# A decoder step on one core: block sums on VectorE instead of GpSimd, squared relu on ScalarE, down products added into the residual rows as they come

## The chip, the core and the metric

The kernel runs on one core of one Trainium2 chip. The core has a matrix engine (TensorE, PE in the profile), VectorE (DVE), ScalarE (ACT) and GpSimd (POOL), each of which takes its own instructions in order; SyncE (SP) issues most transfers between the DRAM and the on-chip memory, in order as well. Matmuls write to PSUM, from which VectorE and ScalarE read. The metric is the device time of one execution in microseconds, the median over runs. Lower is better.

## The reference

One inference step of a decoder layer in fp32, for 1024 prompt tokens and 8 x 8 sample tokens, 1088 tokens in all. The part that matters here is the end of the layer and the output of the updated key and value buffers:

```python
h = x + jnp.einsum('btd,de->bte', mixed, w_o)                       # 1024 -> 1024
z = jnp.einsum('btd,df->btf', rms_norm(h, ln2), w_up)               # 1024 -> 4096
return h + jnp.einsum('btf,fd->btd', jnp.square(jax.nn.relu(z)), w_down)   # 4096 -> 1024
# and, for each of three head groups, the window of keys and values moved on by 8 rows:
kv_s[g].append(jnp.stack([k_full[:, T:], v_full[:, T:]], axis=2))
```

## The kernel before

The products are made of fp32 values split into a high and a low part (`split` and `put`: ScalarE copies the high part, VectorE subtracts it from the value to get the low part), and each product is three matmul passes: high by high, high by low, low by high. Before a matmul can use an operand, both instructions have to have run on it.

The kernel is one long program: input projection, attention and pooling up to about 420 us, gates and the two branch projections to about 660, then the three parts that the change touches.

*w_o.* Two halves of the tokens (`j` = 0, 1; 544 tokens each), each with four weight panels and eight output tiles `y[j][kk]`. Behind each tile its square is added into `sqa[j]`. The first half's norm is woven into the second half's products: the list `todo` has one entry taken behind every half of an output tile, and holds `norm_sums(0)` (matmuls `rth` with ones, then a power on GpSimd), `norm_spread(0)` (matmuls `bc`), the eight `normed` and the eight splits and stores to `u_d`.

*Up.* `w_up` is multiplied block-wise: rows and columns are cut in two, and 7 products of sums and differences of blocks take the place of 8 (the Strassen-Winograd form). `make_versions` makes the sums of activation blocks T1 to T4 from the normalised rows; the weight sums of each of the 16 groups `f` are made in `summed`. A group has 7 steps of 24 matmuls: p1 and p2 need only plain blocks, p5, p6, p7 and p4 need T1, T2, T3 and T4, p3 a plain block. The results of a group are combined, squared (`relu_squared`) and combined again into the seven operands that down wants, and stored to `z_d`. The first `FIRST` groups have their p1 and p2 ahead of everything else, since these need the first half's rows alone; the second half's norm (`norm_sums(1)`, `norm_spread(1)`, `make_versions`) hangs behind the first two of those steps.

*Down.* Seven stages, in the order 2, 4, 1, 5, 6, 7, 3, named after the product they make; each has 16 steps of 24 matmuls into four PSUM tiles (`pd`), which the next stage's first step needs again. A step takes a weight block `w` and a `z` tile. The stages 4 and 1 put their weights into `kept`, and the stages 5, 6, 7 and 3 make sums of blocks on GpSimd (`prep`). `post_down` takes the results out of PSUM behind a stage's last step: into `acs` and `vws` in the stages 2, 4, 1 and 5; behind 6 everything is combined and added to the residual rows `hs`, most of it on GpSimd; behind 7 and 3 the last product is added while the row is written in token order (`finish_row`), and the row is stored.

`run` writes up's and down's steps out: loads are issued 9 steps ahead, `prep` (sums and splits) 3 steps ahead of the matmuls, `post` behind them. PE keeps this order; for the other engines and the transfer queue a scheduler decides how the instructions are interleaved when the program is built. `raw_tile` has two buffers, and in down each holds two steps; five places in turn (`put_up`, `put_down`) hold the split operands, so a split can run as soon as the matmuls of five steps before are done. All loads and stores of these parts go through SP's one queue.

*Copies.* The move of the key and value buffers is 44 copies DRAM to DRAM, issued on GpSimd's queue. Each is made to wait for a mark: the split of a weight panel (`throttle`, one per panel; the last eight are the `w_o` panels) or of an up or down operand (`marks_f`, one per up step, two per down step). The marks are taken at equal distances in one list.

The lines of the profile to know: L1381 and L1382 are the high and low part in `put`, L114 and L115 those in `split`, L1450 the up matmuls, L1722 the down matmuls, L1502 the squared relu, L1540 the weight sums, L1636 the last addition into a row, L1742 the copies; on SP, L1686 loads `hs`, L1691 and L1693 `kept`, L1695 and L1696 `w` and `z`.

Of the kernel before, what the change touches and what calls it, by code (L numbers as in the profile page):

```python
# [32 lines left out]
FIRST = 3  # L33
# [3 lines left out]
def decoder_step(ctx, tc, i, o):  # L37
# [162 lines left out]
    z_d = dp.tile([NG, P, 7, H], F32, name="z_d")  # L200
    new_d = dp.tile([NT, NB, 768], F32, name="new_d")
# [1096 lines left out]
    y = [[pool_.tile([P, H], F32, name=f"y{j}_{k}") for k in range(KD)] for j, pool_ in enumerate((y0p, y1p))]  # L1298
# [34 lines left out]
    for j in range(2):  # L1333
# [32 lines left out]
    up2s = up2 = op = None  # L1366
# [37 lines left out]
    def make_versions():  # L1404

        nonlocal up2s, up2
        nps.close()
        fours = ups.enter_context(tc.tile_pool(name="t4", bufs=1, reuse_waits="tile"))
        sums_at[4] = tuple(fours.tile([P, 4, H], F32R, name=f"t4_{s}") for s in range(2))
        res, rep = right("again")  # L1410
        u12, u22 = y[1][:4], y[1][4:]

        def again(k):
            t = rr(rep, [P, H], F32, name=f"re{k}", tag="re", bufs=4)
            dma(t, u_d[k])
            return t

        def parts(n, k, f):
            hi, lo = (t[:, k, :] for t in sums_at[n])
            split(hi, lo, f)  # L1420

        u11 = [again(k) for k in range(4)]
        for k in range(4):
            normed(k, 1)
            v_.tensor_tensor(u11[k], u12[k], u11[k], op=ALU.subtract)
            parts(1, k, u11[k])
        for k in range(4):
            normed(4 + k, 1)
            split(act[0][4 + k][:, half(1)], act[1][4 + k][:, half(1)], u22[k])
            g_.tensor_tensor(u12[k], u22[k], u12[k], op=ALU.subtract)  # L1430
            v_.tensor_tensor(u22[k], u22[k], u11[k], op=ALU.subtract)
            parts(2, k, u22[k])
        u21 = [again(4 + k) for k in range(4)]
        for k in range(4):
            parts(3, k, u12[k])
        for k in range(4):
            g_.tensor_tensor(u21[k], u21[k], u22[k], op=ALU.subtract)
            parts(4, k, u21[k])
# [15 lines left out]
    queue = []  # L1454
# [8 lines left out]
    def run(ahead=3, load_ahead=9):  # L1463
        n_load = n_prep = 0
        got = {}
        for n in range(len(queue)):
            while n_load < min(len(queue), n + load_ahead):
                if queue[n_load][0]:
                    queue[n_load][0]()
                n_load += 1  # L1470
            while n_prep < min(len(queue), n + ahead):
                got[n_prep] = queue[n_prep][1]()
                n_prep += 1
            queue[n][2](got.pop(n))
            queue[n][3]()

# [30 lines left out]
    def group(f, early):  # L1507
# [11 lines left out]
        def first_post():  # L1519
            t = temp(1, f)  # L1520
            firsts[f] = [t, None, q["x"]]
            s_.copy(two(t), xs_of(q["x"]))  # L1522

        def second_post():
            t = temp(2, f)
# [11 lines left out]

        def summed(n, a, b, op):
            sums[n] = sum_tile(f"{n}_{f}")
            g_.tensor_tensor(by_tile(sums[n]), a, b, op=op)  # L1540
            return put_up(sums[n])

        def p5():
            def post():
# [4 lines left out]
                 lambda A: products(xt(), A, B["T1"], True), post, (lambda: load_panel(f)) if early else None)  # L1549
# [9 lines left out]
        def p7():  # L1559
            def post():  # L1560
# [3 lines left out]
                g_.tensor_tensor(q["s5"], u3, q["s5"], op=ALU.add)  # L1564
# [5 lines left out]
        def p3():  # L1570
            def post():
# [5 lines left out]
                g_.tensor_tensor(t1, z12, z11, op=ALU.subtract)  # L1577
# [3 lines left out]
                g_.tensor_tensor(z12, z22, z12, op=ALU.subtract)  # L1581
# [5 lines left out]
        def p4():  # L1587
            def post():
# [5 lines left out]
                g_.tensor_tensor(t4, z21, q["t2"], op=ALU.subtract)  # L1594
# [19 lines left out]
    kept, acs, vws, hs, rows = {}, {}, {}, {}, {}  # L1614

    def turn_over():
        nonlocal op
# [3 lines left out]
        op = ctx.enter_context(tc.tile_pool(name="down", bufs=1, side="right", reuse_waits="tile"))  # L1621
        for n in (1, 2):
# [5 lines left out]
    def out_row(t, kt, tag):  # L1628
        rows[kt] = op.tile([P, TOK], F32, name=f"row{kt}", tag=f"{tag}.{t}")

    def finish_row(kt, x, js):
        for j in js:
            if x is None:
                s_.copy(by_token(rows[kt], j), two(hs[kt][:, half(j)]))
            else:
                v_.tensor_tensor(by_token(rows[kt], j), two(hs[kt][:, half(j)]), xs_of(x), op=ALU.add)  # L1636

    def post_down(p, xs):
        for t in range(4):
            x = xs_of(xs[t])  # L1640
            if p == 2:
                acs[t] = op.tile([P, 2, H], F32, name=f"ac{t}", tag=f"ac.{t}")
                vws[t] = op.tile([P, 2, H], F32, name=f"vw{t}", tag=f"vw.{t}")
                s_.copy(two(acs[t][:, 0]), x)
            if p == 4:
                s_.copy(two(acs[t][:, 1]), x)
            if p == 1:
                s_.copy(two(vws[t][:, 1]), x)
                v_.tensor_tensor(two(acs[t][:, 0]), two(acs[t][:, 0]), x, op=ALU.add)
            if p == 5:  # L1650
                s_.copy(two(vws[t][:, 0]), x)
            if p == 6:
                a, c, v, w = acs[t][:, 0], acs[t][:, 1], vws[t][:, 0], vws[t][:, 1]
                v_.tensor_tensor(two(w), two(w), x, op=ALU.add)
                g_.tensor_tensor(v, v, w, op=ALU.add)
                g_.tensor_tensor(c, c, w, op=ALU.add)
                for kt, j, s in ((t, 0, a), (t, 1, v), (4 + t, 0, c), (4 + t, 1, v)):
                    (g_ if j else v_).tensor_tensor(hs[kt][:, half(j)], hs[kt][:, half(j)], s, op=ALU.add)  # L1658
                out_row(t, 4 + t, "ac")
                out_row(t, t, "vw")  # L1660
                finish_row(t, None, (0,))
            if p == 7:
                finish_row(4 + t, xs[t], (0, 1))
                dma_st(o["yT"][(4 + t) * P:(5 + t) * P], rows[4 + t])
            if p == 3:
                finish_row(t, xs[t], (1,))
                dma_st(o["yT"][t * P:(t + 1) * P], rows[t])
# [3 lines left out]
    def down_stage(p):  # L1671
# [10 lines left out]
        def load(f):  # L1682
            if f == 0 and p == 5:
                for kt in range(KD):
                    hs[kt] = op.tile([P, TOK], F32, name=f"hs{kt}")
                    dma(hs[kt], h_d[kt])  # L1686
# [11 lines left out]
        def prep(f):  # L1698
# [3 lines left out]
            elif p in (5, 6):  # L1702
                k1 = kept[1, f]
                if p == 5:
                    g_.tensor_tensor(k1, w, k1, op=ALU.add)
                else:
                    g_.tensor_tensor(k1, k1, kept[2, f], op=ALU.subtract)
                w = k1
            elif p == 7:
                g_.tensor_tensor(w, kept[2, f], w, op=ALU.subtract)  # L1710
            elif p == 3:
                g_.tensor_tensor(w, w, kept[1, f], op=ALU.subtract)
# [27 lines left out]
    late = throttle[13:] + marks_f[:-20]  # L1740
# [103 lines left out]
```

## Time and profile before

| | us |
|---|---|
| median of 3 runs (lowest, highest) | 1533.63 (1532.34, 1535.55) |
| the profiled execution, its own time | 1534.52 |
| its span | 1532.7 |
| PE busy in the span | 1459.3 |
| VectorE, ScalarE, GpSimd busy | 937.0, 647.1, 548.4 |
| first up matmul, first and last down matmul | 771.8, 1136.7, 1525.9 |
| mean clock granted to PE | 0.974 of full |

All times within the profile are microseconds from the start of the span, but for means of one instruction, which are in nanoseconds. A group line names line, engine, operation, output and inputs, shape and count, then busy time and mean, then the engine's idle time just before and who ended it. A wait line reads: who waited, for whom, total, times, longest. In a timeline line stand start, duration, the instruction merged with its like, and in brackets the idle time before the first; SPq is SP's queue, on which a transfer's duration is that of its issue and not of the move. A few per cent of the matmul records can be missing.

### The profile page before, as it was taken

Reading aid. Unit: us, or ns where it says so; the run is one execution under the profiler, and the core shown is the slowest. Engines: PE = TensorE matmul, PEld = TensorE weight load, DVE = VectorE, ACT = ScalarE, POOL = GpSimd, SP = SyncE. Lnnn points to the kernel's source line nnn. Section 1 sums busy time; section 2 is a strip of 40 time slices with the busy share of each in tenths; the row PEclk is TensorE's granted clock in tenths of the full one; section 3 lists DMA queues with packets and bytes.
Section 4 is the critical chain, followed back from the end, with each engine's and each line's share of the span. In section 5 each row is a group of like instructions: output and inputs, shape, how many; then the busy total and the mean of one; then the engine's idle time right before and its main releaser. Section 6 shows DMA issues by size and latency. Waiting matters only on the chain. (4 is left out here: it accounts for less than half of the span.)

```text
span 1532.7 us, 28345 instructions
## 1 busy us (share of the span) xinstructions
PE 1459.3 (95%) x10765; PEld 1399.9 (91%) x10765; DVE 937.0 (61%) x1550; ACT 647.1 (42%) x1802; POOL 548.4 (36%) x461
## 2 busy tenths in 40 slices
PE   9999999999999999998988999999999699999788
PEld 8988878888899999998977999999999699999788
DVE  7655575767746424255678766666663346967774
ACT  8567656787433222123342233233333244343331
POOL 1711355455100000000066766665630003825641
PEclk9999999999999999999988999999999799999889
DMA  5312787554354222397534655555579856665483
GB/s 198 107 45 92 215 222 197 146 134 112 112 161 148 81 100 97 100 299 256 207 121 143 213 193 172 192 188 177 196 249 382 309 170 204 221 211 191 163 271 120
DMA packets 160005, 272.69 MB, mean 178 GB/s; under 512 B 32311, under 2 KB 83837, under 8 KB 158142
## 3 DMA queue, kind: packets, MB, share of 16 engines
q1 hardware_dynamic: 153758, 220.56, 45.5%
q0 software_dynamic: 6112, 50.33, 9.9%
q8 instruction: 84, 1.38, 0.4%
q14 instruction: 51, 0.42, 0.1%
HBM read 211.90 MB, written 102.59 MB: 205 GB/s over the span
## 5 line engine op out<-in xcount | busy, mean ns | idle before, releaser
L1722 PE MATMUL pd<-places 128*128 128x272 f32 x2688 | 352.6, 294 | 36.6 <-ACT places L1381 19.9
L1722 PEld LDWEIGHTS pd<-places 128*128 128x128 f32 x2688 | 348.2, 195 | 40.9 <-ACT places L1381 21.7
L1382 DVE TENSOR_TENSOR places<-raw_d,places 128x544 fp32r<-128x544 f32 (+1 forms) x160 | 159.3, 1021 | 61.9 <-ACT places L1381 61.2
L1742 POOL DMA_DIRECT2D out_kv_sample_dram<-in_cache_kv_dram x44 | 22.8, 519 | 419.9 <-ACT places L114 193.5
L1381 ACT ACTIVATE places<-raw_d 128x544 fp32r<-128x544 f32 (+1 forms) x160 | 98.9, 642 | 118.1 <-DMA raw_d<-z_d 53.1
L1450 PE MATMUL pz<-act,places 128*128 128x272 f32 x984 | 133.8, 295 | 8.4 <-DVE act L115 4.3
L1450 PEld LDWEIGHTS pz<-act,places 128*128 128x128 f32 x984 | 130.2, 194 | 9.1 <-DVE act L115 4.7
L1382 DVE TENSOR_TENSOR places<-kept,places 128x512 fp32r<-128x512 f32 x64 | 55.6, 869 | 82.4 <-ACT places L1381 82.3
L184 PE MATMUL pga<-act,places 128*128 128x384 f32 (+1 forms) x576 | 100.2, 333 | 0.0
L184 PE MATMUL ph<-act,places 128*128 128x272 f32 x768 | 99.3, 292 | 0.6 <-ACT places L114 0.6
L184 PEld LDWEIGHTS ph<-act,places 128*128 128x128 f32 x768 | 98.6, 192 | 0.9 <-ACT places L114 0.8
L184 PE MATMUL pgb<-act,places 128*128 128x384 f32 (+1 forms) x576 | 97.9, 327 | 0.0
L184 PEld LDWEIGHTS pga<-act,places 128*128 128x128 f32 x576 | 96.2, 190 | 0.8 <-issue 0.3
L184 PEld LDWEIGHTS pgb<-act,places 128*128 128x128 f32 x576 | 95.4, 188 | 0.0
L599 POOL TENSOR_TENSOR mr<-ms,mhalf 128x4 f32<-128x4 f32 (+2 forms) x39 | 52.3, 1343 | 108.1 <-DVE ms L598 107.9
L1381 ACT ACTIVATE places<-kept 128x512 fp32r<-128x512 f32 x64 | 40.4, 632 | 114.3 <-PE pd L1722 73.4
L1450 PE MATMUL pz<-act,apart 128*128 128x272 f32 x552 | 74.2, 293 | 2.5 <-ACT t L1522 2.5
L1450 PEld LDWEIGHTS pz<-act,apart 128*128 128x128 f32 x552 | 72.2, 192 | 2.8 <-ACT t L1522 2.7
L1502 DVE SCALAR_TENSOR_TENSOR t<-t 128x544 f32<-128x544 f32 x48 | 55.2, 1150 | 18.8 <-POOL t L1564 18.8
L804 POOL TENSOR_TENSOR pck<-pck,qs 128x256 f32<-128x256 f32 x64 | 48.1, 783 | 43.0 <-DMA pck<-in_cache_kv_dram 17.5
L1540 POOL TENSOR_TENSOR sm<-raw_u 128x512 f32<-128x512 f32 x32 | 52.4, 1637 | 29.3 <-DVE places L1382 15.3
L184 PE MATMUL pqk<-places,act 128*128 128x512 f32 x240 | 61.0, 403 | 1.0 <-ACT qk L604 1.0
(371 smaller groups left out, 2922.5 us busy)
## 6 DMA issues: line engine op xcount, KB each, us to landing
out_kv_sample_dram<-in_cache_kv_dram POOLq DMA_DIRECT2D x36, 960.0 KB, 6.3
raw_d<-z_d SPq DMA_DIRECT2D x112, 272.0 KB
z_d<-t SPq DMA_DIRECT2D x96, 272.0 KB
raw_u<-in_w_up_dram SPq DMA_DIRECT2D x64, 256.0 KB
raw_d<-in_w_down_dram SPq DMA_DIRECT2D x64, 256.0 KB
raw_qkv<-in_w_in_dram SPq DMA_DIRECT2D x36, 256.0 KB
xr<-in_xT_dram SPq DMA_DIRECT2D x8, 1088.0 KB
pck<-in_cache_kv_dram SPq DMA_DIRECT2D x32, 256.0 KB
```

Of the source, the lines that this page charges most:

```text
L184: last_mm[0] = t_.matmul(out, lhs(a, k), rhs(b, k), start=(j == 0), stop=(j == len(terms) - 1))
L599: g_.tensor_tensor(r[:n, :H], ms[:n, :H], mhalf[:n, :H], op=ALU.pow)
L804: behind_pe(g_.tensor_tensor(t[:, n], t[:, n], qs[:, :256], op=ALU.mult))
L1381: ins = s_.activation(view(t[:, 0]), src, AF.Copy)
L1382: v_.tensor_tensor(view(t[:, 1]), src, view(t[:, 0]).bitcast(F32), op=ALU.subtract)
L1450: t_.matmul(x[:, c, :Q], A[:, a, k * P:(k + 1) * P], Bv(b, k, c), start=(first and n == 0), stop=(n == len(terms) - 1), skip_group_check=n ...
L1502: v_.scalar_tensor_tensor(t, t, 0.0, t, op0=ALU.max, op1=ALU.mult)
L1540: g_.tensor_tensor(by_tile(sums[n]), a, b, op=op)
L1722: t_.matmul(q["x"][t][:, c, :Q], A[:, a, t * P:(t + 1) * P], Z[:, b, c * Q:(c + 1) * Q], start=(f == 0 and n == 0), stop=(f == NG - 1 and ...
L1742: ins = g_.dma_start(d, a)
```

## The change

All sums of weight blocks and of results move from GpSimd to VectorE; the squared relu becomes two ScalarE passes. `FIRST` goes from 3 to 5; the early groups' two results are parked in `e` tiles, written out to `p_d` and `z_d` and read back when the group goes on. `make_versions` works on two blocks (1088 columns) at a time. The first half's norm is taken two half-tiles later, and its spread three. In down, `hs` is loaded beside the last eight steps of stage 2 instead of ahead of stage 5; the results are added to `hs` as they come, one addition behind a step (`later`), and `acs` and `vws` are replaced by `parked` and `running`. The marks of the copies count the panels several times, and down's marks singly and without the first 24.

```diff
-FIRST = 3
+FIRST = 5
...
+    p_d = dp.tile([FIRST, P, H], F32, name="p_d")
...
-            todo += [lambda: norm_sums(0), lambda: norm_spread(0)]
+            wait = lambda: None
+            todo += [wait, wait, lambda: norm_sums(0), wait, lambda: norm_spread(0)]
...
+        u12, u22 = fours[1]
+        u11 = rep.tile([P, 4, H], F32, name="u11")
+        pairs = (slice(0, 2), slice(2, 4))
+        def minus(out, a, b):
+            for k in pairs:
+                v_.tensor_tensor(out[:, k], a[:, k], b[:, k], op=ALU.subtract)
+        def parts(hi, lo, f):
+            for k in pairs:
+                split(hi[:, k], lo[:, k], f[:, k])
+        for k in range(4):
+            dma(u11[:, k], u_d[k])
         for k in range(4):
             normed(k, 1)
+        minus(u11, u12, u11)
+        parts(*sums_at[1], u11)
+        for k in range(4, 8):
+            normed(k, 1)
+        minus(u11, u22, u11)
+        parts(*sums_at[2], u11)
+        minus(u12, u22, u12)
+        parts(*sums_at[3], u12)
+        parts(plane(0, 1, 1), plane(1, 1, 1), u22)
         for k in range(4):
+            dma(u12[:, k], u_d[4 + k])
+        minus(u12, u12, u11)
+        parts(*sums_at[4], u12)
...
             queue[n][3]()
+            if later:
+                later.pop(0)()
...
-        return rr(up if n < 3 else up2, [P, H], F32, name=f"t{n}_{name}", tag=f"t{n}", bufs=FIRST if n < 3 else 1)
+        return rr(up if n < 3 else up2, [P, H], F32, name=f"t{n}_{name}", tag=f"t{n}", bufs=2 if n < 3 else 1)
+    def park(n, name):
+        return rr(up, [P, H], F32, name=f"e{n}_{name}", tag=f"e{n}", bufs=1)
     def relu_squared(t):
-        v_.scalar_tensor_tensor(t, t, 0.0, t, op0=ALU.max, op1=ALU.mult)
+        s_.activation(t, t, AF.Relu)
+        s_.activation(t, t, AF.Square)
...
+            if early:
+                dma_st(p_d[f], t)
...
+        def back():
+            load_panel(f)
+            for n, src in ((1, p_d[f]), (2, z_d[f, :, 0, :])):
+                firsts[f][n - 1] = temp(n, f"again{f}")
+                dma(firsts[f][n - 1], src)
         def summed(n, a, b, op):
             sums[n] = sum_tile(f"{n}_{f}")
-            g_.tensor_tensor(by_tile(sums[n]), a, b, op=op)
+            v_.tensor_tensor(by_tile(sums[n]), a, b, op=op)
...
-                g_.tensor_tensor(q["s5"], u3, q["s5"], op=ALU.add)
+                v_.tensor_tensor(q["s5"], u3, q["s5"], op=ALU.add)
...
+    def adds(kt, j, src):
+        return lambda: v_.tensor_tensor(hs[kt][:, half(j)], hs[kt][:, half(j)], src, op=ALU.add)
+    def row_half(kt, j, src):
+        v_.tensor_tensor(by_token(rows[kt], j), two(hs[kt][:, half(j)]), src, op=ALU.add)
...
+            v, w = parked[:, t], running[:, t]
+            if p in (2, 4):
+                kt = t if p == 2 else 4 + t
+                v_.tensor_tensor(two(hs[kt][:, half(0)]), two(hs[kt][:, half(0)]), x, op=ALU.add)
             if p == 1:
+                s_.copy(two(w), x)
+                later.append(adds(t, 0, w))
             if p == 5:
+                s_.copy(two(v), x)
+                later.extend((adds(t, 1, v), adds(4 + t, 1, v)))
             if p == 6:
                 v_.tensor_tensor(two(w), two(w), x, op=ALU.add)
+                later.extend((adds(4 + t, 0, w), adds(t, 1, w), adds(4 + t, 1, w)))
             if p == 7:
+                s_.copy(two(v), x)
+                new_row(4 + t)
+                later.append(lambda t=t, v=v: row_half(4 + t, 0, two(v)))
+                later.append(lambda t=t, v=v: (row_half(4 + t, 1, two(v)), row_done(4 + t)))
             if p == 3:
+                row_half(t, 1, x)
+                row_done(t)
+        if p == 7:
+            for t in range(4):
+                later.append(lambda t=t: (new_row(t), s_.copy(by_token(rows[t], 0), two(hs[t][:, half(0)]))))
...
-            if f == 0 and p == 5:
-                for kt in range(KD):
-                    hs[kt] = op.tile([P, TOK], F32, name=f"hs{kt}")
-                    dma(hs[kt], h_d[kt])
+            if p == 2 and f >= KD:
+                kt = f - KD
+                hs[kt] = op.tile([P, TOK], F32, name=f"hs{kt}")
+                dma(hs[kt], h_d[kt])
...
-                    g_.tensor_tensor(k1, w, k1, op=ALU.add)
+                    v_.tensor_tensor(k1, w, k1, op=ALU.add)
...
-    late = throttle[13:] + marks_f[:-20]
+    n_up = 7 * NG
+    late = [t for t in throttle[13:-8] for _ in range(4)] + [t for t in throttle[-8:] for _ in range(2)]
+    late += marks_f[:n_up] + marks_f[n_up + 24:-20:2]
```

The three other sums in `prep` (`kept[1]` less `kept[2]`, `kept[2]` less `w`, `w` less `kept[1]`) and the four other sums of results in up change their engine in the same way. `new_row` gives the rows `4 + t` and `t` the same buffer, so row `t` waits for the store of row `4 + t`.

More of the change, by code (lines that the diff above doesn't have):

```diff
@@ L1611, in decoder_step @@
                 p()
-    kept, acs, vws, hs, rows = {}, {}, {}, {}, {}
+    kept, hs, rows = {}, {}, {}
     def turn_over():
-        nonlocal op
+        nonlocal op, parked, running
         ups.close()
@@ L1621, in turn_over @@
         op = ctx.enter_context(tc.tile_pool(name="down", bufs=1, side="right", reuse_waits="tile"))
+        parked, running = (op.tile([P, 4, H], F32, name=n) for n in ("parked", "running"))
         for n in (1, 2):
@@ L1638, in post_down, with new_row, row_done @@
+    def row_half(kt, j, src):
+        v_.tensor_tensor(by_token(rows[kt], j), two(hs[kt][:, half(j)]), src, op=ALU.add)
+    def new_row(kt):
+        rows[kt] = op.tile([P, TOK], F32, name=f"row{kt}", tag=f"row.{kt % 4}")
+    def row_done(kt):
+        dma_st(o["yT"][kt * P:(kt + 1) * P], rows[kt])
     def post_down(p, xs):
+        assert not later
         for t in range(4):
             x = xs_of(xs[t])
[L1641 to L1644, printed above, removed]
```

76 lines of the change are left out of this document (15 added, 61 removed).

## The prediction

> **What bounds the kernel now.** I read the page's first part, then TensorE (PE) stage by stage, then what PE waited for.
>
> ```profile
> span 1532.7 us, 28345 instructions
> PE 1459.3 (95%) x10765; PEld 1399.9 (91%) x10765; DVE 937.0 (61%) x1550; ACT 647.1 (42%) x1802; POOL 548.4 (36%) x461
> ...
> 860.00:1100.00 240.00, 240.00 (x1913) 240.00 (x1913) 164.02 (x173) 74.81 (x124) 151.84 (x103) 1.00 0.54 183
> 1222.00:1292.00 70.00, 70.00 (x564) 70.00 (x564) 32.85 (x47) 29.55 (x51) 6.20 (x8) 1.00 0.57 188
> ...
> 771.80:826.30 54.50, 39.96 (x232) 37.95 (x231) 45.48 (x52) 24.13 (x42) 35.41 (x20) 0.78 0.42 138
> 1136.60:1185.30 48.70, 48.24 (x386) 47.85 (x384) 24.55 (x33) 17.74 (x30) 6.31 (x6) 1.00 0.98 355
> 1185.30:1256.00 70.70, 55.13 (x411) 54.31 (x411) 25.65 (x38) 25.76 (x44) 2.43 (x5) 0.88 0.71 251
> 1300.00:1353.00 53.00, 48.56 (x374) 47.94 (x373) 49.09 (x41) 19.59 (x34) 41.60 (x30) 0.97 0.65 217
> 1403.00:1466.00 63.00, 52.58 (x378) 51.30 (x378) 51.99 (x38) 21.32 (x32) 47.30 (x34) 0.92 0.54 180
> 1466.00:1525.90 59.90, 54.18 (x393) 52.88 (x392) 33.90 (x39) 16.64 (x28) 18.91 (x15) 0.89 0.52 171
> ...
> PE pd L1722 <- ACT places L1381: 19.9, 3, 11.5
> PE pz L1450 <- ACT t L1522: 6.5, 2, 4.1
> PE pd L1722 <- DVE row L1636: 5.7, 4, 2.8
> PE pd L1722 <- DVE places L1382: 4.5, 5, 2.5
> PE pd L1722 <- DVE ac L1649: 4.3, 2, 2.5
> PE pz L1450 <- DVE act L115: 4.3, 2, 3.7
> ...
> 721.85 2.03 PE L1309 MATMUL rth<-ones,sqa 128*128 128x1 f32 x10 [4.56 <-DVE sqa L1353]
> 723.81 5.31 PE L184 MATMUL ph<-act,places 128*128 128x272 f32 x24
> ...
> 774.81 1.14 PE L1309 MATMUL rth<-ones,sqa 128*128 128x1 f32 x10
> 779.24 1.16 PE L1322 MATMUL bc<-dg,ones 128*128 128x272 f32 x4
> ```
>
> A window row holds, after its length, busy time and count of PE, weight loads, VectorE (DVE), ScalarE (ACT) and GpSimd (POOL), then PE's clock, the DMA share and GB/s. Where nothing disturbs it PE is the bound, at clock 1.00: 1913 matmuls in 240 us are a step of 24 in 3.01 us (up), 564 in 70 us one in 2.98 us (down). I price the count of each disturbed window at that rate; what is over is lost time:
>
> - the first half's norm: 4.56 us of wait, and 24 matmuls in 5.31 us instead of 2.98: 6.9;
> - the start of up (771.8): 232 less 14 of the norm are 218, or 27.3 us, plus 2.3 us for those 14: 24.9 of the 54.5;
> - the start of down: 386 are 47.9 of 48.7 us, 411 are 51.0 of 70.7: 0.8 + 19.7;
> - its boundaries at 1300, 1403 and 1466: 374 are 46.4 of 53.0, 378 are 46.9 of 63.0, 393 are 48.8 of 59.9: 6.6, 16.1 and 11.1.
>
> Together 86 us. Without them the profiled run's own 1534.5 us would be 1448, a floor, since the change issues the same matmuls. The tail (last matmul near 1526, end 1532.7) stays.
>
> **Sums from POOL to VectorE, squares to ScalarE.** The same VectorE shapes, first with POOL at work (1320 to 1345), then with POOL nearly still (1210 to 1284), and other durations that I use:
>
> ```profile
> L1382 DVE TENSOR_TENSOR places<-raw_d,places 128x544 fp32r<-128x544 f32 x8 | 16.1, 2016 | 0.0
> L1382 DVE TENSOR_TENSOR places<-kept,places 128x512 fp32r<-128x512 f32 x7 | 9.5, 1354 | 2.0 <-ACT places L1381 1.8
> ...
> L1382 DVE TENSOR_TENSOR places<-raw_d,places 128x544 fp32r<-128x544 f32 x26 | 18.6, 720 | 0.4 <-ACT places L1381 0.4
> L1382 DVE TENSOR_TENSOR places<-kept,places 128x512 fp32r<-128x512 f32 x24 | 16.6, 692 | 40.3 <-ACT places L1381 40.3
> ...
> L115 DVE TENSOR_TENSOR mx<-sga,mx 128x384 fp32r<-128x384 f32 x12 | 6.7, 559 | 9.7 <-ACT mx L114 9.7
> ...
> L1590 DVE TENSOR_TENSOR t<-t,pz 128x544 f32<-128x544 f32 x12 | 8.7, 721 | 9.3 <-PE pz L1450 9.3
> L1527 ACT ACTIVATE t<-t 128x544 f32<-128x544 f32 x11 | 7.3, 660 | 0.3
> ...
> L1636 DVE TENSOR_TENSOR row<-hs,pd x12: 1111/1130/1176, 1467.6 to 1526.5; 128x544 f32<-128x544 f32 x12
> ```
>
> A subtraction of 512 columns takes 692 ns, beside POOL's sums 1354; one of 544 takes 720 against 2016. A moved sum thus costs VectorE 0.69 to 0.72 us and gives 0.65 to 1.3 us back on its neighbours. For an up group (7 steps, 21.1 us): before, 164.02 of 240 us, or 14.4 us; after, 7 splits, 4 sums, 4 adds out of PSUM and 5 other adds, 20 operations at about 0.71: 14.2 us. ScalarE gains six passes of 0.66 us, 4.0 us on 6.6 (74.81 of 240), so it is half busy. I leave the up steps at 3.01 us: weights are prepared three to four steps, some 9 us, ahead. With that cover gone each late VectorE operation would cost PE 0.7 us.
>
> In down, per stage of 16 steps (47.7 us of PE), the built order puts most of the sums of stages 5 and 6 into stage 5: 32 splits, 32 sums and 4 adds, 68 operations, 48 us. Stage 7: 32 splits, 16 sums, 12 adds and 4 adds out of PSUM: 45 us. Stage 3: 48, and 8 row halves of 1.13 us: 43 us. VectorE is 90 to 100% full there: it keeps pace, without reserve.
>
> The Trainium skill has a rule against this part: Perfetto Trace Analysis, section Optimizing Scalar/DVE Operations, would relieve a saturated VectorE by ScalarE or even GpSimd, though it adds that GpSimd shares a read port with it, so that this might not help. By its first half stages 5, 7 and 3 lose their reserve, which is the second rival's ground; by its caveat they gain, and 692 against 1354 ns sides with that.
>
> **Five groups begun early.** Behind the second norm PE now has 8 steps (24 us) before the first sum is used, not 4 (12 us). By the built order VectorE owes until the second sum (T2) is split: 8 normalisations and 9 operations of 512 columns at 0.7 us, and 15 of 1088 columns at 1.28 (from 559 to 692 ns over 128 columns, 1.0 ns a column): 31 us. PE wants the last of T2 28 us after the norm's broadcast. So 3.5 us of gaps (0 if ScalarE's and PE's waits fall well; 9 if a 1088 costs two 720s and the reload of u_d is late). What a gap adds in clock, and the start of down on SP's queue:
>
> ```profile
> 785.88 4.81 PE L1450 MATMUL pz<-act,apart 128*128 128x272 f32 x24 [2.46 <-ACT t L1522]
> ...
> 1171.57 8.77 SPq L1693 DMA_DIRECT2D kept<-in_w_down_dram  x11
> 1180.63 4.47 SPq L1696 DMA_DIRECT2D raw_d<-z_d  x2
> 1185.15 2.34 SPq L1693 DMA_DIRECT2D kept<-in_w_down_dram  x5
> 1187.65 6.55 SPq L1686 DMA_DIRECT2D hs<-h_d  x8
> 1195.28 19.20 SPq L1696 DMA_DIRECT2D raw_d<-z_d  x8
> 1208.59 0.60 PE L1722 MATMUL pd<-places 128*128 128x272 f32 x1 [11.46 <-ACT places L1381]
> ...
> 1141.00:1181.00 40.00, 40.00 (x324) 40.00 (x323) 19.49 (x26) 14.68 (x25) 4.38 (x5) 1.00 1.06 384
> ...
> out_kv_sample_dram<-in_cache_kv_dram POOLq DMA_DIRECT2D x36, 960.0 KB, 6.3
> ```
>
> Behind a gap of 2.46 us, 24 matmuls took 4.81 us: 1.8 us lost again. I add 2.5 us: 6 left of 24.9 (0 to 14). TensorE: Matmul & The Clock Gate (Trainium skill, section What's actually happening) lets the clock fall only after an idle window of some 3.4 us; by that 3.5 would be left instead of 6, but the row shows a shorter gap that pays.
>
> The early groups' two parked tiles go out to p_d and z_d and come back, 15 DMAs more of 272 KB. They lie beside 183 GB/s of 384; a reload waits on SP's queue for its store, and behind it stands an up panel that is wanted several steps later. Nothing is priced.
>
> **Norm.** The sums of squares move two half-tiles (6 us) later, past the 4.56 us of wait, and their spread one more half-tile. On POOL's queue a copy now stands ahead of the norm's power; it waits for a weight split of about the same moment. 1 left of 6.9 (0 to 7).
>
> **Copies and loads.** Counted from the two lists of marks, 3 of 44 copies hang on weight panels before and 10 after; on down's marks 26 and 15, and the first 24 marks of down, which carried three, carry none. Two more (960 KB, 2.5 us of DMA at 384 GB/s) fall among the panels of w_o: 2 us lost (0 to 5).
>
> At the start of down the rows show the stall: 8 hs loads stand before z loads, and PE resumes 13 us after those were issued. Now hs comes in stage 2. By the built order 8 hs (544 KB), 23 kept tiles (256 KB) and 16 w,z loads go in a row up to the last pair of stage 2: 14.8 MB, 39 us at 384 GB/s. They start when the last z stores are issued, two adds and four ScalarE passes after up ends (1136.6), at about 1142, and end at 1181, the last pair from 1178; PE wants it at 1179. Besides, three of stage 4's splits now stand ahead of it on ScalarE and wait for PE. 3 us; then 9 kept tiles and the first z, perhaps a copy (7 to 10 us) against two steps and a boundary: 3 more; clock 3: 9 left of 20.5 (3 to 21).
>
> **Results added one per step.** At 1403 and 1466 go the clump on POOL and VectorE and the two row halves (1.13 us each) that held PSUM. Stage 7 now begins with four adds out of PSUM, others sorted between them: by the built order 3.6 us of gaps, with clock 5 left of 16.1 (2 to 12). Stage 3 begins with ScalarE copies, as stages 1 and 6 do without loss now: 2 left of 11.1 (0 to 6: its row copies wait on ScalarE for the stores of earlier rows, and splits stand behind them). Stage 5 likewise: 1 of 6.6. Stages 4 and 1 begin with VectorE adds instead of copies: 1.
>
> **Sum.** Left: 6 + 1 + 2 + 9 + 5 + 2 + 1 + 1 = 27. 1448 + 27 = 1475 against the profiled 1534.5; the median shown is 0.9 lower: 1474.
>
> **Rivals.**
> 1. Loads and waits, not POOL, set the gaps: the start of down keeps 20, the start of up 14, 1403 and 1466 half (13), the rest 6: 53 left, 1500. For it: 384 GB/s is reached from 1141 on already, and 4.4 MB come in earlier. Against: three copies leave that stretch, and VectorE was full (49.09 of 53.0, 51.99 of 63.0 us) where the late boundaries lost.
> 2. Slower: a sum on VectorE waits for its DMA and every split behind it waits too, where POOL waited alone. Stages 5, 7 and 3 have 48 steps and no reserve; from 1.25 us a step on, the 60 gained are gone; at 2 us it is 1474 + 96 = 1570. Against: in the built order four to seven operations (3 to 5 us) lie between a tile's last split and the next sum that needs it.
> 3. Almost nothing is left over: 10, 1457. For it: the cover of 9 us behind every split.
>
> **How the numbers follow.** Forecast 0.65 (own range 1461 to 1490), rivals 0.17, 0.09 and 0.09. The range 1457 to 1500 ends in the middle of the first and third, which leaves out some 0.2. A measurement tells 0.2% (3 us) from no change. Slower is the second rival's upper part, 0.08; same 0.01; faster 0.91.
>
> **What would show it.** POOL busy behind 780 us with copies alone; VectorE's 512 and 544 columns at 0.69 and 0.72 us throughout; no wait of PE over 6 us near 1190; steps of 3.01 and 2.98 us. Wrong if sums in stages 5, 7 and 3 show VectorE idle until a DMA and PE steps above 3.3 us, or if the start of down still loses 20.

## The result, and the profile after

| | before | after |
|---|---|---|
| median (runs) | 1534.59 us (4) | 1495.69 us (4: 1490.15 to 1499.66) |
| ratio to before, 95% interval | | 0.9744 [0.9709, 0.9779] |
| profiled execution, its span | 1534.5, 1532.7 us | 1495.8, 1494.0 us |
| mean granted clock of TensorE | 0.974 | 0.986 |

The change saves 38.9 us where 60 were forecast: the time lies in the range of 1457 to 1500 us, 21.7 us above its point and outside the forecast's own 1461 to 1490. The first part of the page after, and what PE waited for:

```profile
span 1494.0 us, 28199 instructions
PE 1442.5 (97%) x10765; PEld 1386.0 (93%) x10765; DVE 899.7 (60%) x1704; ACT 702.0 (47%) x1884; POOL 204.4 (14%) x245
...
PE pz L1454 <- ACT e L1532: 9.3, 4, 4.7
PE pd L1741 <- ACT places L1384: 8.4, 2, 6.1
PE ph L184 <- ACT places L114: 5.1, 1, 5.1
PE pz L1454 <- DVE t L1591: 4.1, 1, 4.1
```

Two of the longest waits are new: 5.1 us on a w_o panel and 4.1 us on an add of up (L1591). The windows of the disturbed stretches, in the columns of the prediction:

```profile
689.00:768.80 79.80, 75.34 (x584) 75.16 (x585) 46.49 (x65) 27.55 (x44) 2.57 (x4) 0.96 0.68 239
768.80:820.00 51.20, 41.84 (x294) 40.54 (x293) 40.77 (x48) 26.72 (x39) 3.59 (x5) 0.90 0.72 229
...
875.00:889.00 14.00, 9.93 (x59) 9.74 (x59) 7.71 (x12) 4.77 (x8) 0.00 (x0) 0.76 0.49 162
889.00:1129.90 240.90, 240.90 (x1921) 240.90 (x1920) 151.55 (x231) 119.40 (x199) 6.34 (x13) 1.00 0.61 204
1129.90:1172.00 42.10, 42.02 (x338) 41.80 (x336) 17.13 (x26) 14.99 (x26) 0.00 (x0) 1.00 1.02 374
1172.00:1190.00 18.00, 9.17 (x51) 8.44 (x52) 7.26 (x11) 5.38 (x9) 0.98 (x2) 0.79 1.02 380
1190.00:1238.00 48.00, 48.00 (x378) 48.00 (x378) 23.51 (x37) 19.56 (x33) 0.98 (x2) 0.97 0.47 152
...
1286.00:1334.00 48.00, 48.00 (x388) 48.00 (x387) 38.93 (x64) 21.62 (x37) 1.46 (x3) 1.00 0.65 215
...
1382.20:1390.00 7.80, 4.36 (x29) 3.70 (x29) 7.71 (x13) 1.49 (x3) 0.49 (x1) 1.00 0.64 203
...
1432.00:1445.00 13.00, 10.09 (x79) 9.65 (x78) 9.25 (x13) 6.35 (x11) 0.00 (x0) 1.00 0.44 138
1445.00:1487.40 42.40, 41.03 (x328) 40.59 (x326) 28.23 (x42) 16.00 (x24) 0.00 (x0) 1.00 0.48 169
```

Each count priced as in the prediction (24 matmuls at 3.01 us in up, 2.98 elsewhere, 2.3 us for the norm's 14) gives the time lost. For instance 875 to 889: 59 are 7.4 us of 14, so 6.6 are lost; 768.8 to 820: 280 are 35.1, with the norm 37.4 of 51.2, so 13.8. From 689 to 768.8, 570 are 70.8, with the first half's norm 73.1 of 79.8, so 6.7.

| lost, us | before | forecast | after |
|---|---|---|---|
| w_o panels | 0 | 2 | 6.7 |
| first norm | 6.9 | 1 | 0 |
| start of up | 24.9 | 6 | 13.8 |
| up near 880 | 0 | 0 | 6.6 |
| start of down | 20.5 | 9 | 12.8 |
| start of stage 5 | 6.6 | 1 | 0 |
| start of stage 7 | 16.1 | 5 | 4.2 |
| start of stage 3 | 11.1 | 2 | 4.9 |
| starts of stages 4, 1 | 0 | 1 | 0 |
| sum | 86 | 27 | 49.0 |

1448 and 49.0 are 1497.0, against 1495.8 (some matmul records are missing, which counts as loss). The rows behind the entries, timeline first for the start of up (start, duration, and in brackets the idle time with what ended it):

```profile
793.34 0.35 SPq L1515 DMA_DIRECT2D z_d<-e  x1
800.59 0.62 ACT L1538 ACTIVATE e<-pz 128x544 f32<-128x544 f32 x1 [7.13 <-DMA z_d<-e]
801.81 0.59 ACT L1532 COPY e<-pz 128x544 f32<-128x544 f32 x1
802.46 8.29 PE L1454 MATMUL pz<-act,apart 128*128 128x272 f32 x48 [4.65 <-ACT e L1532]
```

The parking tile `e2` is one buffer: ScalarE's relu for the next group waits until the store of the last group has landed, the copy out of PSUM stands behind it on ScalarE, and PE behind that. Near 880:

```profile
870.69 4.47 SPq L1491 DMA_DIRECT2D raw_u<-in_w_up_dram  x2
...
881.13 0.69 DVE L1558 TENSOR_TENSOR sm<-raw_u 128x512 f32<-128x512 f32 x1 [8.25 <-DMA raw_u<-in_w_up_dram]
881.86 0.69 DVE L1558 TENSOR_TENSOR sm<-sm,raw_u 128x512 f32<-128x512 f32 x1
882.47 0.71 DVE L1591 TENSOR_TENSOR t<-t_again,pz 128x544 f32<-128x544 f32 x1
...
883.33 5.73 PE L1454 MATMUL pz<-places 128*128 128x272 f32 x24 [4.07 <-DVE t L1591]
```

Two weight sums of the sixth group (`f` = 5) wait on VectorE for its panel; the add that empties a PSUM tile of the fourth stands behind them. At stage 3 the same shape, over two engines:

```profile
1437.96 0.69 DVE L1731 TENSOR_TENSOR raw_d<-raw_d,kept 128x512 f32<-128x512 f32 x1 [2.00 <-DMA raw_d<-in_w_down_dram]
1438.77 0.63 ACT L1384 ACTIVATE places<-raw_d 128x512 fp32r<-128x512 f32 x1 [2.46 <-DVE raw_d L1731]
1439.30 0.59 ACT L1677 COPY parked<-pd 128x544 f32<-128x544 f32 x1
...
1439.95 10.10 PE L1741 MATMUL pd<-places 128*128 128x272 f32 x79 [2.11 <-ACT parked L1677]
```

The fourth copy out of PSUM stands behind a split that waits for a sum that waits for a transfer. The Trainium skill (TensorE: Matmul & The Clock Gate, section Architectural detail: the array is 16× 32×32, not 1× 128×128) says that ScalarE and VectorE take their queue strictly in order; these rows agree.

### The profile page after: what moved, and what is told of

It is laid out like the page before. It is cut to its first block, busy times and chain, and to the rows that moved or that the text cites. A ratio compares the mean times of both kernels' runs of the same rounds, so it can differ in the third digit from the quotient of the medians.

```text
span 1494.0 us, 28199 instructions
## 1 busy us (share of the span) xinstructions
PE 1442.5 (97%) x10765; PEld 1386.0 (93%) x10765; DVE 899.7 (60%) x1704; ACT 702.0 (47%) x1884; POOL 204.4 (14%) x245
## 5 line engine op out<-in xcount | busy, mean ns | idle before, releaser
L1741 PE MATMUL pd<-places 128*128 128x272 f32 x2688 | 340.8, 289 | 16.5 <-ACT places L1384 8.4
L1741 PEld LDWEIGHTS pd<-places 128*128 128x128 f32 x2688 | 338.3, 190 | 19.0 <-ACT places L1384 11.1
L1385 DVE TENSOR_TENSOR places<-raw_d,places 128x544 fp32r<-128x544 f32 (+1 forms) x160 | 109.7, 711 | 32.5 <-ACT places L1384 32.2
L1454 PE MATMUL pz<-act,places 128*128 128x272 f32 x912 | 119.5, 289 | 2.8 <-ACT e L1532 2.8
L1454 PEld LDWEIGHTS pz<-act,places 128*128 128x128 f32 x912 | 116.5, 188 | 3.3 <-ACT e L1532 3.2
L1454 PE MATMUL pz<-act,apart 128*128 128x272 f32 x624 | 85.9, 297 | 6.6 <-ACT e L1532 6.6
L1454 PEld LDWEIGHTS pz<-act,apart 128*128 128x128 f32 x624 | 83.5, 196 | 7.1 <-ACT e L1532 7.0
L1385 DVE TENSOR_TENSOR places<-kept,places 128x512 fp32r<-128x512 f32 x64 | 44.1, 689 | 65.1 <-ACT places L1384 65.0
L1454 PE MATMUL pz<-places 128*128 128x272 f32 x432 | 58.9, 295 | 4.1 <-DVE t L1591 4.1
L1454 PEld LDWEIGHTS pz<-places 128*128 128x128 f32 x432 | 57.4, 196 | 4.3 <-issue 4.3
L184 PEld LDWEIGHTS pqk<-places,act 128*128 128x128 f32 x240 | 44.6, 192 | 11.1 <-ACT qk L605 1.2
```

The source lines that it names most:

```text
L184: last_mm[0] = t_.matmul(out, lhs(a, k), rhs(b, k), start=(j == 0), stop=(j == len(terms) - 1))
L1385: v_.tensor_tensor(view(t[:, 1]), src, view(t[:, 0]).bitcast(F32), op=ALU.subtract)
L1454: t_.matmul(x[:, c, :Q], A[:, a, k * P:(k + 1) * P], Bv(b, k, c), start=(first and n == 0), stop=(n == len(terms) - 1), skip_group_check=n ...
L1741: t_.matmul(q["x"][t][:, c, :Q], A[:, a, t * P:(t + 1) * P], Z[:, b, c * Q:(c + 1) * Q], start=(f == 0 and n == 0), stop=(f == NG - 1 and ...
```

## The experiments

Theory after the result: the change's gain is PE time that the clump of adds, the row halves and the start of up had cost; what it gave back is instructions that wait for a transfer ahead of others that free PSUM. Rivals: the engine of the sums is the gain (contention with GpSimd); or the bytes moved set the gaps.

### Which part gives the gain

`results_alone` is the kernel before with the new `post_down`, `later`, `hs` in stage 2, and nothing else.

> The kernel before with only the handling of the down results changed: the residual rows loaded in the first down stage, one add into them per step, the last products parked by ScalarE; sums on GpSimd, squares on VectorE, three early groups and the old copies. Theory (the clump of adds and the row halves held PSUM and made the late losses, whichever engine makes the sums): of 33.8 us at the boundaries 1300, 1403 and 1466 some 24 go, the start of down keeps 13 to 20 of its 20.5: about 1507 us (1503 to 1512). Rival (only together with the sums on VectorE, since GpSimd's sums slow the added VectorE work too): 1520 or more, VectorE's subtractions at 1.0 us and more.

Measured 1509.83 us, ratio 0.9855 [0.9813, 0.9896]: some 22 of the 39 us, as the theory had it. All of it lies in down, which takes 365.4 us from its first matmul to its last instead of 389.2; up stays at 364.6 (before 364.9). The edit moves the loads of `hs` too, but PE's waits at the start of down are 14.4 us after 15.1, so the gain is in the boundaries, while GpSimd still makes the sums.

`sums_alone` is the kernel before with

```
-            g_.tensor_tensor(by_tile(sums[n]), a, b, op=op)
+            v_.tensor_tensor(by_tile(sums[n]), a, b, op=op)
...
-                g_.tensor_tensor(w, w, kept[1, f], op=ALU.subtract)
+                v_.tensor_tensor(w, w, kept[1, f], op=ALU.subtract)
```

and so for each block sum, and the squares on ScalarE.

> The kernel before with only the sums of up, of the down stages and of the second half's versions moved from GpSimd to VectorE and the squares to ScalarE; copies, early groups, hs loads and the clump of adds behind stage 6 are as before. Theory (VectorE was slowed by GpSimd's sums): its 512-column subtraction shows 0.69 us throughout; of the 33.8 us lost at the boundaries 1300, 1403 and 1466 some 12 go, the clump and the row halves keep the rest; the starts of up and of down keep their 25 and 20: about 1522 us, ratio 0.992. Rival A (a sum on VectorE waits for its transfer with the splits behind it): no gain or a loss, 1534 to 1550, with waits of VectorE on a DMA ahead of PE's. Rival B (the sums are nearly all of the gain): 1505 or less.

Measured 1531.13 us, ratio 0.9986 [0.9972, 1.0]: a gain of 0 to 0.3%, some 9 us short of the theory. The timeline of its last boundary shows why:

```profile
1463.20 0.69 DVE L1713 TENSOR_TENSOR raw_d<-raw_d,kept 128x512 f32<-128x512 f32 x1 [2.92 <-DMA raw_d<-in_w_down_dram]
...
1467.10 2.07 DVE L1637 TENSOR_TENSOR row<-hs,pd 128x544 f32<-128x544 f32 x2
...
1469.32 1.70 PE L1723 MATMUL pd<-places 128*128 128x272 f32 x6 [13.98 <-DVE row L1637]
```

With the old row halves reading PSUM, sums that wait for transfers ahead of them cost PE 14 us at once, and six waits for late splits in down another 10.5. Up, from its first matmul to the first of down, became 5.2 us shorter (359.7 instead of 364.9), and down 3.8 longer (393.0 instead of 389.2). At the boundaries near 1300 and 1403, where the theory looked for its gain, PE's waits for results hardly fell (3.7 and 1.2 us, before 4.3 and 1.6). The reverse, the kernel after with only the sums of stages 5, 6, 7 and 3 back on GpSimd:

> The changed kernel with only the weight sums of the down stages 5, 6, 7 and 3 back on GpSimd. Theory (GpSimd slows VectorE where VectorE is full): the subtractions go back to 1.3 to 2 us in stages 5 and 6 and behind 7, boundaries lose again: about 1510 us (1502 to 1522). Rival A (VectorE's in-order waits on transfers cost more than the contention): 1490 or less.

Measured 1498.6 us, ratio 0.978 [0.9745, 0.9816]: no difference from the kernel after that the intervals would show. The theory had asked for 1502 us or more and the rival for 1490 or less; neither came. The groups by form, 1300 to 1400 us, first after, then here:

```profile
L1385 DVE TENSOR_TENSOR places<-raw_d,places 128x544 fp32r<-128x544 f32 x32 | 23.0, 717 | 0.0
```

```profile
L1385 DVE TENSOR_TENSOR places<-raw_d,places 128x544 fp32r<-128x544 f32 x33 | 35.0, 1062 | 0.0
```

Beside GpSimd's sums the subtraction does take 1062 instead of 717 ns, but PE's waits in down grew by nothing: the added time was covered. And with only the sums of up back on GpSimd:

> The changed kernel with only the sums of up (weight sums and results) back on GpSimd. Theory: the steps of up are covered either way, and what the move cost there is the stall near 883 us, where VectorE waited 8 us in a weight sum for its panel and held up an add out of PSUM (6.6 us): about 1490 us (1486 to 1496). Rival B (contention matters in up too): 1503 or more.

Measured 1493.35 us, ratio 0.9743 [0.9722, 0.9765], the same time as after. The stall of 4.07 us on L1591 is gone, with 0.9 and 2.3 us on ScalarE in its place, and the wait at the parking tile was 7.5 us in this run instead of 4.65. What is left of the 39 us, some 15 by difference from `results_alone` and `sums_alone` if the parts add, belongs to the five early groups, the norm's place and the copies; these were not run alone.

### The start of up

`keep2` leaves the first two early groups in the tiles that they are used from; only groups 2 to 4 pass through the parking tiles:

```
-            t = (park if early else temp)(1, f)
+            t = (park if early and f > 1 else temp)(1, f)
...
-            if early:
+            if early and f > 1:
                 dma_st(p_d[f], t)
...
-            for n, src in ((1, p_d[f]), (2, z_d[f, :, 0, :])):
+            for n, src in ((1, p_d[f]), (2, z_d[f, :, 0, :])) if f > 1 else ():
```

> The changed kernel in which the first two of the five early groups stay in the tiles that they are used from, instead of passing through the single parking tiles: two stores and four reloads fewer, and groups 2 to 4 alone share the parking tiles. Theory (ScalarE waited for the parking tile's store, 7.1 us behind one of them, and PE for ScalarE): the gaps of 1.9 and 4.7 us at the start of up go, with 2 us of clock: 1488 us. Rival (ScalarE is full of splits there and the stores hide nothing): the gaps move, 1494 to 1497.

Measured 1491.29 us, ratio 0.9733 [0.9717, 0.975]. PE's timeline there, and last ScalarE ahead of the third gap:

```profile
781.04 3.29 PE L1454 MATMUL pz<-act,apart 128*128 128x272 f32 x24 [0.71 <-ACT t L1532]
...
796.84 6.30 PE L1454 MATMUL pz<-act,apart 128*128 128x272 f32 x48 [1.78 <-ACT e L1532]
...
796.18 0.61 ACT L1532 COPY e<-pz 128x544 f32<-128x544 f32 x1 [2.44 <-DMA p_d<-e]
```

The four gaps are 0.71, 1.42, 1.78 and 1.46 us instead of 1.91, 1.31, 4.65 and 1.46, and the clock is no longer lost (48 matmuls behind the third in 6.30 us, in the kernel after 8.29; the granted clock from 767 to 820 us is 1.00). The parking tile's store is shown as the cause of the long one: the third gap is 4.65 to 7.52 us in the five kernels in which all five groups pass through the tiles, and 0.70 to 2.05 in the six in which two do not. The intervals of the whole times overlap; the gaps are what tells. Of what stays, the 1.78 us still stand behind the other parking tile, for whose store to `p_d` ScalarE waited 2.44 us.

### The stall near 880

`keep2_late` asks for the reloads later, so that they do not stand on SP ahead of the next panel (`again_late` is the loop over `p_d` and `z_d` of `keep2`, hung on the step with B["22"]):

> The kernel with the first two early groups kept (keep2), and in groups 2 to 4 the two reloads are asked for four steps later, when their tiles are about free, so that they no longer stand on SP's queue ahead of the next panel. Theory (SP waited 5.5 us with a reload whose tile was in use, the next panel behind it came late, VectorE waited for it in a weight sum): the stall of 4.1 us near 880 goes, with its clock: 1485 us. Rival (the panel is late because a cache copy of 960 KB and the stores took the DMA engines): it stays, 1490 to 1492.

Measured 1487.58 us, ratio 0.9696 [0.9666, 0.9726]; but the stall stayed at 3.25 us: the reloads on SP's queue are not its cause. `z21_first` leaves the panel as it is and orders VectorE:

```
-            v_.tensor_tensor(by_tile(sums[n]), a, b, op=op)
+            ins = v_.tensor_tensor(by_tile(sums[n]), a, b, op=op)
+            if n in (1, 3) and f > 1:
+                behind_pe(ins, z21s[f - 2])
...
-                v_.tensor_tensor(two(z21), two(z21), xs_of(q["x7"]), op=ALU.add)
+                z21s[f] = v_.tensor_tensor(two(z21), two(z21), xs_of(q["x7"]), op=ALU.add)
```

> keep2_late with one more edit: the weight sums of an up group may not start on VectorE until the last add out of PSUM of the group two before is done (in the kernel after, the first sums of the sixth group stand ahead of that add and wait for their panel). Theory (order on VectorE: the sum waits for its transfer and the add behind it holds PSUM): the stall near 872 us goes whole though the panel is no earlier, 1487.6 - 4 to 5: 1483 us. Rival (the panel itself is too late for PE): the stall comes back some steps later as a wait for places, 1487.

Measured 1483.3 us, ratio 0.9667 [0.9636, 0.9698] (it overlaps that of `keep2_late`; the wait is what tells), and no wait of PE between 815 and 1160 us. VectorE at that place:

```profile
871.78 0.72 DVE L1612 TENSOR_TENSOR t_again<-t_again,pz 128x544 f32<-128x544 f32 x1
...
874.29 1.29 DVE L1560 TENSOR_TENSOR sm<-raw_u 128x512 f32<-128x512 f32 x2
```

The sums start after the add, without a wait: PE needs the first of them at 889.6 us, five steps later. The order on VectorE was the cause, not the panel.

### The w_o panels

The transfers issued from 655 to 694 us, before and then after (size and, where known, the median to landing):

```profile
raw_o<-in_w_o_dram SPq DMA_DIRECT2D x14, 256.0 KB
...
raw_uf<-in_w_up_dram SPq DMA_DIRECT2D x6, 256.0 KB
```

```profile
raw_o<-in_w_o_dram SPq DMA_DIRECT2D x11, 256.0 KB
raw_uf<-in_w_up_dram SPq DMA_DIRECT2D x8, 256.0 KB
...
out_kv_sample_dram<-in_cache_kv_dram POOLq DMA_DIRECT2D x1, 960.0 KB, 7.9
```

A copy and two more first quarters of early groups (`raw_uf`) stand where three w_o loads stood. `no_o` takes the copy away:

```
-    late = [t for t in throttle[13:-8] for _ in range(4)] + [t for t in throttle[-8:] for _ in range(2)]
+    late = [t for t in throttle[13:-8] for _ in range(4)]
```

> The changed kernel without the two copies that hang on the w_o panels; they are spread over the other marks. Theory (one copy of 960 KB put back a stretch in which the DMA engines are full from 676 to 694 us): the gap of 5.1 us near 693 goes, with 2 us of clock: 1488 to 1490 us. Rival (the row stores and the panels fill that stretch by themselves): the gap stays, 1495.

Measured 1495.67 us, ratio 0.9752 [0.9725, 0.9779]. The wait near 693 went from 5.13 to 1.42 us, as the theory had it: the same stretch of time holds 14 w_o loads again, beside the eight `raw_uf`. The whole did not move: in this run the first wait at the start of down (7.70 instead of 6.15 us) and those of stage 7 (4.75) and of the third gap of up (5.77) were longer. That these are the same copies in a new place was not tried.

### The start of down

> The changed kernel with the residual rows 0 to 3 asked for in the last four steps of stage 2, and rows 4 to 7 in the last four of stage 4, each just ahead of its use. Theory (the bytes decide the start of down: 2.2 MB fewer ahead of the last pair of stage 2 are 5.8 us at 384 GB/s): the gap of 6.1 us near 1178 shrinks to 1 or 2, 1490 us. Rival (the order on SP's queue decides, z loads behind rows wherever these are): the gap moves behind, 1494 to 1497.

The edit moves `hs` to the steps 12 to 15 of stages 2 and 4. Measured 1499.41 us, ratio 0.9764 [0.9737, 0.9791]: the first gap fell from 6.15 to 2.31 us and the second rose from 2.23 to 6.94. So both hold in part: with four rows fewer ahead of it the last pair of stage 2 came sooner, as the theory had it, and the loss moved behind, as the rival had it. SP's timeline in the kernel after:

```profile
1158.80 6.50 SPq L1710 DMA_DIRECT2D kept<-in_w_down_dram  x10
1165.64 5.30 SPq L1712 DMA_DIRECT2D kept<-in_w_down_dram  x7
1171.64 0.33 SPq L1714 DMA_DIRECT2D raw_d<-in_w_down_dram  x1
```

The kept tiles have buffers of their own, so their loads wait for nothing and stand 17 in a row ahead of the last pair of stage 2, though PE wants them one a step, some 45 to 85 us later. `paced` ties each to a matmul:

```
+    def ask_kept(t, src):
+        if t is not None:
+            asked.append((t, src))
+        if len(asked) > 2 or t is None and asked:
+            behind_pe(dma(*asked.pop(0)), at_pe[0])
...
-                dma(kept[1, f], of(f, 1, 1))
+                ask_kept(kept[1, f], of(f, 1, 1))
...
-                dma(kept[2, f], of(f, 0, 0))
+                ask_kept(kept[2, f], of(f, 0, 0))
...
-                        t_.matmul(q["x"][t][:, c, :Q], A[:, a, t * P:(t + 1) * P], Z[:, b, c * Q:(c + 1) * Q],
+                        at_pe[0] = t_.matmul(q["x"][t][:, c, :Q], A[:, a, t * P:(t + 1) * P], Z[:, b, c * Q:(c + 1) * Q],
```

> keep2_late with the loads of the kept weight tiles of down stages 4 and 1 each tied to a matmul some six steps ahead of its use; in the kernel after, 23 of them (256 KB each) were issued ahead of the last weight pair of stage 2. Theory (the last pair stood on SP's queue behind 17 kept loads that filled the DMA engines): the last pair is issued some 6 us earlier, the gaps of 5.6 and 2.1 us at the start of down shrink to 0 to 2: 1487.6 - 8: 1480 us. Rival (eight residual rows and the pairs alone fill the engines there): the gaps stay, 1486 to 1489.

Measured 1475.78 us, ratio 0.9622 [0.9582, 0.9661]: 11.8 us from one reordering of transfers, against 8 expected. PE and the DMA share there:

```profile
1120.00:1165.00 45.00, 45.00 (x364) 45.00 (x363) 24.05 (x36) 20.98 (x34) 0.49 (x1) 1.00 0.95 342
1165.00:1185.00 20.00, 20.00 (x163) 20.00 (x162) 11.72 (x18) 8.27 (x14) 0.49 (x1) 1.00 0.75 250
```

PE has no wait at all at the start of down, with the same bytes in all.

### Together

> Both edits of z21_first and paced on keep2_late. If the two places are independent the gains add: 1476 us (1473 to 1480). Rival (time won in one place is given back where transfers are late, since their sum of bytes is fixed): 1481 or more.

Measured 1466.99 us, ratio 0.9569 [0.9542, 0.9597], better than the 1476 expected and than the two gains added (4.3 and 11.8 from 1487.6 would be 1471.5); with intervals of 8 to 12 us that is no contradiction. The longest of its waits of PE behind 660 us:

```profile
PE ph L184 <- ACT places L114: 4.4, 1, 4.4
PE pz L1454 <- ACT e L1532: 3.6, 3, 1.5
PE pd L1755 <- DVE running L1678: 3.0, 1, 3.0
PE pd L1755 <- ACT parked L1681: 2.8, 2, 2.1
```

The last kernel adds two edits for the first, third and fourth of these:

```
+            if f < 4:
+                behind_pe(ins, throttle[-3])
...
+            if p in (7, 3) and f in (4, 5):
+                behind_pe(ins, held[0])
```

(`ins` is the load of a first quarter panel, then the weight sum; `held[0]` the last add or copy out of PSUM of the stage before.)

> The kernel of both with two more edits, each read in its own place. First: the eight loads of up's first quarter panels (256 KB each, issued from 663 us on between the w_o panels, 80 us ahead of their use) wait for a late w_o split; the copy near 664 us stays. If these loads filled the stretch, the wait of 4.4 us near 693 falls under 1; if the copy alone does it, it stays above 3. Second: in stages 7 and 3 the weight sums of the steps 4 and 5 may not start before the last result of the stage before is out of PSUM (they stood ahead of it, waiting for their transfer): the waits of 3.0 and 2.1 us near 1357 and 1412 go to 1 or less each. Together 1467 - 9: 1458 us (1454 to 1463); if the losses only move, 1465 or more.

Measured 1467.81 us, ratio 0.9555 [0.953, 0.958], the same as `both`. Each wait aimed at in the first edit and at stage 7 went: 4.4 to 0.3 us near 693, 3.0 to 0.7 at stage 7; at stage 3 2.07 stayed. But the norm's wait came back:

```profile
726.34 0.63 ACT L114 ACTIVATE places<-raw_o 128x512 fp32r<-128x512 f32 x1 [4.54 <-DMA raw_o<-in_w_o_dram]
...
727.84 0.64 ACT L1354 ACTIVATE hq<-y 128x544 f32<-128x544 f32 x1
...
729.44 1.58 PE L1311 MATMUL rth<-ones,sqa 128*128 128x1 f32 x10 [4.03 <-DVE sqa L1355]
```

The last square of the norm stands on ScalarE behind w_o splits that wait 4 us and more for their loads. The loss moved by 35 us, as the rival had it; why those loads were late was not tried.

## Why the prediction was right or wrong

The time fell in the range, but not because the sum was right: 27 us were to be left, 49.0 were, and the large misses all go the same way. What carries the range past 1490 is the weight given to the first rival, so that the time lies in it is partly luck.

- **What bounds it, and the ledger: right.** Steps stayed at 3.01 and 2.98 us (240.9 us for 1921 matmuls), and the price by count accounts for the profiled 1495.8 within 2 us.
- **Sums to VectorE: durations right, worth little.** 0.69 and 0.72 us were forecast, 684 to 727 ns measured, and POOL issues copies only. But `sums_alone` gives 0 to 0.3%, and `pool_down` shows that 1062 ns in their place cost PE nothing that can be told: a slower VectorE had cover. That a moved sum gives time back on its neighbours was true and carried none to PE. The count of VectorE's work was too high besides: 48, 45 and 43 us in stages 5, 7 and 3 were forecast, "without reserve", and 38.9, 36.9 and 37.5 measured, since operations in a row cost less than their durations added (four of 512 columns at 1433 took 2.56 us).
- **Results one per step: right.** It is the largest part (`results_alone`, 22 us, without any sum moved). The three boundaries were forecast to go from 33.8 to 8 and went to 9.1; stage 3 kept 4.9 instead of 2, mostly by the fourth copy behind a waiting split; the bound "0 to 6" covered it.
- **Five early groups: the term that was mis-sized most.** 6 us left were forecast, 13.8 measured. The 3.5 us of gaps were worked out from what VectorE owed; it was ScalarE that was late, most of all at parking tiles with one buffer, and the gaps came to 9.3 us. The prediction looked at the 15 added transfers on SP's queue and at DMA bytes, wrote "Nothing is priced", and did not ask who waits for a store. `keep2` showed it for the long gap and for the clock behind it; 5.4 us of gaps stayed.
- **"I leave the up steps at 3.01 us": failed at one place.** 6.6 us near 880. This is the second rival's mechanism, set down for stages 5, 7 and 3 only; in up, the built order has two sums of the next panel ahead of an add out of PSUM. `z21_first` showed that the order was the cause.
- **Copies: 2 us forecast (0 to 5), 6.7 measured.** The price was the copies' own time in the DMA engines; what was lost is a wait of 5.1 us for a w_o panel and the clock behind it. The two more `raw_uf` loads that five groups bring into the same stretch were not counted. Taking the copy away (`no_o`, 1.42 us of wait left) and holding all eight `raw_uf` loads back (`last`, 0.29) each clears it; that the two added ones alone matter was not tried.
- **Norm: right.** 1 forecast, 0 measured.
- **Start of down: size near (9 forecast, 12.8 measured), reason right as far as it went.** The sum was of the bytes in a row ahead of the last pair, and the DMA engines were full there (a share of 1.02, 374 GB/s). The first gap was 6.15 us where 3 were forecast, just over the 6 that the prediction had set as a sign. The order it took as given: 17 of these loads were for tiles that PE wanted 45 us later or more. `hs_split` took bytes away there and the loss moved; `paced` kept the bytes in all and removed it.
- **Rivals.** The first (loads and waits set the gaps, 1500 us) came nearest in time, and half by its mechanism: transfers do set most of what is left, by what stands ahead of them or waits with them in a queue rather than by the sum of their bytes; its start of up (14) is what was measured, its start of down (20) is not. The second acted near 880 and at stage 3 and is far from making the kernel slower.

## What to carry to other kernels

When work moves to an engine with a queue in order, read in the built order what stands behind each instruction that waits for a transfer; if that frees PSUM, tie the waiting one behind it (some 4 us here). A load whose buffer is free is issued as early as its queue allows and delays the one wanted next: tie it to the consumer's progress (12 us here). Where a tile through which values pass to a store has one buffer, the store's landing becomes a wait on the engine that fills it (7.13 us here); `keep2` kept two groups out of the tiles, and a second buffer was not tried.

## What the runs showed of the hardware

**The clock's price for short gaps.** Twenty-four matmuls behind a wait of PE, in `pool_down`, after and `results_alone`:

```profile
784.87 3.29 PE L1454 MATMUL pz<-act,apart 128*128 128x272 f32 x24 [1.88 <-ACT e L1532]
```

```profile
782.36 4.81 PE L1454 MATMUL pz<-act,apart 128*128 128x272 f32 x24 [1.91 <-ACT e L1532]
```

```profile
782.54 4.80 PE L1450 MATMUL pz<-act,apart 128*128 128x272 f32 x24 [2.10 <-ACT t L1524]
```

A gap of 1.88 us cost nothing more, gaps of 1.91 and 2.10 us each 1.5 us of slower matmuls behind them; but behind the 2.11 us at 1439.95 above, 79 matmuls took 10.10 us, near the 9.8 of full rate, and in `keep2_late` the same 79 took 11.64 us behind 2.15. So around 2 us both occur. The Trainium skill (TensorE: Matmul & The Clock Gate, section What's actually happening) lets the clock fall after an idle window of about 3.4 us that runs free of the kernel: that the phase decides agrees with rows so close together, that shorter gaps pay does not.
